# Laying out SBUF by hand in a two-layer streaming trunk, with every block chain of matmuls 256 columns wide

## The chip, the cores and the metric

The kernel runs on one core of a Trainium2 chip. The metric is the device time of one execution in microseconds. Of the kernel before there are three timed runs and one profiled execution.

## What is computed

The reference is a trunk of two layers over 512 tokens of width 1024, in float32. Layer A mixes tokens with a chunkwise mLSTM and a memory attention, layer B with a banded attention on a shared K/V projection and the memory attention. Each has a gated MLP with a depthwise convolution (inner width 2816) behind it.

```python
def conv_ffn(h, w_up, conv_w, conv_b, w_down):
    u, g = jnp.split(h @ w_up, 2, axis=-1)
    g = causal_dwconv(g, conv_w, conv_b)
    return (jax.nn.silu(g) * u) @ w_down

# layer A: x + [mlstm_chunkwise | memory_attention](rmsnorm(x) @ w_in) @ w_out
# layer B: x + [band_attention | memory_attention](rmsnorm(x) @ w_in) @ w_out, with one shared K/V projection
# each layer then: x + conv_ffn(rmsnorm(x)); after layer B a final rmsnorm
```

The change concerns the two MLPs most, since each has its matrix products done there in blocks of 256 tokens.

## The kernel before

**Number format.** Every matrix is split into a high part (a cast to fp32r on ScalarE, L130) and a low part (a subtraction on VectorE, L131). A product is three matmuls, high by high, high by low, low by high (`mm3`, L177, L178, L179). The weight, the stationary operand, is loaded into TensorE for every matmul; the activations move. In the profile's names `wh` and `wl` are the high and the low part of a weight, `u` is a tile of any split activation, query, block form or state, and `pmm`, `psc`, `ptr` are PSUM tiles.

**The channel mixer (the MLP).** It runs over 22 output tiles j of 128 features. Tiles 0 to 4 (`plain`) are 512 columns wide. Tiles 5 to 21 are written as `later()` and `step()`: a step computes the up and the gate product of one tile for both halves of the tokens with seven calls in place of eight, by sums and differences of weight quarters and of the token halves. The calls, in the order of the program, are a11, a12, s2, then one unit of down products, s1, s3, a second unit, a22, s4. A call has four k-tiles, each with three matmuls of 256 columns, so 12 matmuls. The stationary operands of a11 and a12 are the parts of the up weights (`split_up`), those of s1 and s3 the parts of sums (`split_sums`), all four in `wh` and `wl` tiles. Those of s2, a22 and s4 are "forms" (`form`), split into two tiles with the tag `u` each. A down unit has 12 matmuls of 512 columns into `ptr`. Steps 5 to 8 have one unit, 9 to 20 two, 21 none. There are 17 steps in each of the two layers, 34 in all.

**Wide steps.** In steps 9 to 20 (`WIDE`, 24 of the 34) the calls s2, s3 and a22 are done by `wide_products`: for each k one matmul of 256 columns with the low part (L792) and one of 512 columns with the high part (L793), whose moving operand is the high and the low half of the activation side by side. The half of the result that lies in columns 256 to 511 of the bank is added afterwards on VectorE (L829).

**Order.** In the block stages the order on PE, ACT and DVE is that in which `later` and `step` are written, pinned by a manual schedule. Elsewhere a scheduler orders instructions by priority, and tags with a number of buffers decide when a tile is free again: an allocation takes the next buffer of its tag in turn and waits until that buffer's last reader is done. The DMA loads are on SP's queue in program order.

**Places in SBUF.** The pool has a tag for each kind of tile: `wr` (raw weights, 3 of 4096 bytes a partition), `wh` and `wl` (3 each, D + 64 floats, that is 4352 bytes or 8.5 times 512), `u` (57 of 2048 bytes), `t`, `pt`, `s`, `rb`, `bias`. The up parts and the sums begin 16 floats (`SHIFT`, 64 bytes) into their tile. In the built program every moving operand of the block stages begins at the same place modulo 512 bytes. Counted from there, the stationary forms lie at 0, and the parts of up and sums at 64 or at 320: since a tile is 8.5 times 512 bytes long, neighbours of one tag differ by 256, and where `wh` lies at 64, its `wl` lies at 320, and the other way round. The down weights and the weights of the plain stage lie at 0 or 256.

The lines that the change and the prediction's steps touch: the pool's sizes (L82), `small` (L95), `weight_tiles` and `parts` (L150 to L161), `form`, `split_up` and `split_sums` (in `Forms`, L862 on), `sum_products` and `later` (L795 to L829), x's tiles (in `reload_x`, L423), and the queries of layer B.

## Time and profile before

| what | value |
|---|---|
| median of 3 runs (lowest to highest) | 1190.41 us (1190.38 to 1190.46) |
| the profiled execution's own time | 1191.35 us |
| its span (first to last instruction) | 1189.6 us |
| mean granted TensorE clock | 0.999 |
| block stage of layer A, first matmul to the end | 341.87 to 587.8 us |
| block stage of layer B | 900.6 to 1146.8 us |

The profile is of one execution, on its own clock from the first instruction of the span. A row of its groups has line, engine, operation, output <- inputs, shapes, how often it occurs, busy time in us, mean ns of one, and the time that the engine stood idle just before it, with what ended that. In a timeline row the first two numbers are start and duration in us. A matmul's duration holds its way through the array and overlaps the next one's, so what a matmul costs is the distance from its start to the next start.

### The profile page before, as it was taken

Reading aid. Unit: us, or ns where it says so; the run is one execution under the profiler, and the core shown is the slowest. Engines: PE = TensorE matmul, PEld = TensorE weight load, DVE = VectorE, ACT = ScalarE, POOL = GpSimd, SP = SyncE. Lnnn points to the kernel's source line nnn. Section 1 sums busy time; section 2 is a strip of 40 time slices with the busy share of each in tenths; the row PEclk is TensorE's granted clock in tenths of the full one; section 3 lists DMA queues with packets and bytes.
Section 4 is the critical chain, followed back from the end, with each engine's and each line's share of the span. In section 5 each row is a group of like instructions: output and inputs, shape, how many; then the busy total and the mean of one; then the engine's idle time right before and its main releaser. Section 6 shows DMA issues by size and latency. Waiting matters only on the chain.

```text
span 1189.6 us, 18184 instructions
## 1 busy us (share of the span) xinstructions
PE 1179.0 (99%) x6719; PEld 1032.1 (87%) x6719; DVE 961.9 (81%) x1760; ACT 723.6 (61%) x1294; POOL 130.0 (11%) x222
## 2 busy tenths in 40 slices
PE   9999999999999999999999999999999999999997
PEld 8988888888889988999888888888889988999986
DVE  6877688888978888888798888997896888888855
ACT  5648677655655555555576667776565655555545
POOL 1211201010021111111021000101001010111100
PEclk9999999999999999999999999999999999999999
DMA  8645313444266666666564313245326466665551
GB/s 283 212 114 133 93 55 80 146 142 135 87 160 159 158 162 158 154 145 132 145 197 131 89 53 102 70 131 184 117 89 152 107 141 142 142 141 137 123 159 71
DMA packets 200155, 158.61 MB, mean 133 GB/s; under 512 B 8344, under 2 KB 179838, under 8 KB 200066
## 3 DMA queue, kind: packets, MB, share of 16 engines
q1 hardware_dynamic: 183906, 119.74, 34.3%
q0 software_dynamic: 15584, 36.67, 15.3%
q8 instruction: 53, 0.87, 0.3%
q10 hardware_dynamic: 576, 1.05, 0.2%
q14 instruction: 36, 0.29, 0.1%
HBM read 128.89 MB, written 32.46 MB: 136 GB/s over the span
## 4 chain that ended last, share of the span: by engine, by line
PE 92%; ACT 3%; DVE 2%; DMA 2%; issue 0%; SPq 0%; POOL 0%; POOLq 0%; DVEq 0%; ACTq 0%
PE pmm L177 15%; PE pmm L178 15%; PE pmm L179 14%; PE ptr L178 6%; PE ptr L177 6%; PE ptr L179 6%; PE pmm L793 6%; PE psc L179 5%; PE psc L178 5%; PE psc L177 5%; PE pmm L792 3%; PE psc L527 2%; DMA wr<-in_mem_w_kv_dram 2%; PE ptr L1358 1%; PE ptr L1379 1%; PE ptr L1380 1%
## 5 line engine op out<-in xcount | busy, mean ns | idle before, releaser
L177 PE MATMUL pmm<-u,wh 128*128 128x512 f32 (+1 forms) x872 | 307.6, 353 | 0.3 <-ACT u L130 0.2
L179 PE MATMUL pmm<-u,wl 128*128 128x512 f32 (+1 forms) x872 | 304.7, 350 | 0.0
L178 PE MATMUL pmm<-u,wh 128*128 128x512 f32 (+1 forms) x872 | 304.6, 350 | 0.0
L131 DVE TENSOR_TENSOR wl<-wr,wh 128x1024 fp32r<-128x1024 f32 (+3 forms) x172 | 199.8, 1162 | 56.8 <-ACT wh L130 54.9
L130 ACT CAST wh<-wr 128x1024 fp32r<-128x1024 f32 (+3 forms) x172 | 171.8, 1001 | 98.4 <-PE pmm L178 44.3
L179 PEld LDWEIGHTS pmm<-u,wl 128*128 128x128 f32 x872 | 163.9, 188 | 21.0
L177 PEld LDWEIGHTS pmm<-u,wh 128*128 128x128 f32 x872 | 164.3, 189 | 18.5 <-ACT u L130 1.1
L178 PEld LDWEIGHTS pmm<-u,wh 128*128 128x128 f32 x872 | 164.2, 188 | 18.2 <-DVE u L131 0.5
L177 PE MATMUL ptr<-u,wh 128*128 128x512 f32 x272 | 106.7, 392 | 0.0
L178 PE MATMUL ptr<-u,wh 128*128 128x512 f32 x272 | 106.2, 390 | 0.0
L179 PE MATMUL ptr<-u,wl 128*128 128x512 f32 x272 | 106.0, 390 | 0.0
L761 POOL DMA_DIRECT2D xspill<-t x64 | 55.5, 867 | 454.2 <-ACT t L760 443.5
L130 ACT CAST u<-pt 128x512 fp32r<-128x512 f32 x102 | 62.7, 617 | 46.9 <-DVE pt L883 46.8
L131 DVE TENSOR_TENSOR u<-pt,u 128x512 fp32r<-128x512 f32 x102 | 69.9, 688 | 11.0 <-ACT u L130 8.3
L177 PE MATMUL psc<-u,wh 128*128 128x256 f32 (+1 forms) x232 | 75.9, 327 | 0.0
L179 PE MATMUL psc<-u,wl 128*128 128x256 f32 (+1 forms) x232 | 75.7, 326 | 0.0
L178 PE MATMUL psc<-u,wh 128*128 128x256 f32 (+1 forms) x232 | 75.6, 326 | 0.0
L793 PE MATMUL pmm<-u,u 128*128 128x512 f32 x192 | 69.9, 398 | 0.0
L945 ACT ACTIVATE t<-t 128x512 f32<-128x512 f32 x34 | 21.5, 633 | 79.4 <-DVE t L668 79.4
L829 DVE TENSOR_TENSOR t<-t,pmm 128x256 f32<-128x256 f32 x72 | 30.1, 419 | 41.8 <-ACT t L827 41.8
L760 ACT COPY t<-ptr 128x512 f32<-128x512 f32 x64 | 37.4, 585 | 42.9 <-PE ptr L179 42.8
L668 DVE SCALAR_TENSOR_TENSOR t<-t,cols,t 128x511 f32<-128x511 f32 x80 | 59.7, 746 | 3.7 <-ACT t L675 3.7
(300 smaller groups left out, 2670.6 us busy)
## 6 DMA issues: line engine op xcount, KB each, us to landing
wr<-in_ffn_w_up_dram SPq DMA_DIRECT2D x54, 512.0 KB, 4.2
wr<-in_ffn_w_down_dram SPq DMA_DIRECT2D x38, 512.0 KB, 4.1
pt<-in_ffn_w_up_dram SPq DMA_DIRECT2D x34, 512.0 KB, 6.4
xspill<-t POOLq DMA_DIRECT2D x64, 256.0 KB, 5.3
wr<-in_a_w_in_dram SPq DMA_DIRECT2D x20, 512.0 KB, 3.8
xspill<-u POOLq DMA_DIRECT2D x32, 256.0 KB, 2.7
u<-xspill SPq DMA_DIRECT2D x32, 256.0 KB, 4.8
wr<-in_w_kv_dram SPq DMA_DIRECT2D x12, 512.0 KB, 3.8
```

What stands on the lines that cost most here:

```text
L130: high = A.copy(hi, src) if on_act else V.tensor_copy(hi, src)
L131: low = V.tensor_tensor(out=lo, in0=src, in1=f(hi), op=ALU.subtract)
L177: nc.tensor.matmul(o, lh, rh, start=first, stop=False, skip_group_check=more)
L178: nc.tensor.matmul(o, lh, rl, start=False, stop=False, skip_group_check=more)
L179: nc.tensor.matmul(o, ll, rh, start=False, stop=last, skip_group_check=more)
L527: nc.tensor.matmul(o, a, b, start=first and i == 0, stop=i == 1)
L668: V.scalar_tensor_tensor(acc[:, n:], src[:, : S - n], self.fw[:, c * FT + j : c * FT + j + 1], acc[:, n:], op0=ALU.mult, op1=ALU.add,)
L760: A.copy(t, o)
L761: G.dma_start(xspill[j], t, accum_op=ALU.add)
L792: nc.tensor.matmul(r[:, :H], w[1][:, k], p[i - 1][:, :H], start=False, stop=False, skip_group_check=True)
L793: nc.tensor.matmul(r, w[0][:, k], p[i - 1], start=False, stop=k == n - 1, skip_group_check=True)
L829: V.tensor_tensor(out=o, in0=o, in1=r[:, H:], op=ALU.add)
```

## The change

Three things are changed together.

1. **Places.** The pool's tags are laid out in a fixed order (`sizes`, with one `first_` tile of each tag allocated ahead). `wh` and `wl` become six tags of one buffer each, `wh0` to `wh2` and `wl0` to `wl2`. Up parts always take block 0 and sums always block 1, both 16 floats in; all other weights take the next block in turn. The small vectors `s0` to `s3` lie between them and fill each block up to a multiple of 512 bytes. A new tag `f` of eight tiles takes the forms, the tiles of x (`xT`), the queries of layer B's first five head pairs and of one memory pair, which all had `u` tiles; `u` has 50 buffers instead of 57. In the built program the moving operands begin where they began modulo 512, and counted from there every stationary operand of the seven calls lies at 64, forms included, and those of the down and plain products at 0.
2. **Width.** `WIDE` and `wide_products` are gone: all seven calls of all 34 steps are 12 matmuls of 256 columns, with no addition on VectorE behind them. TensorE has 288 matmuls more (72 calls, 12 in place of 8), VectorE has 72 instructions fewer.
3. **Constants.** `ones` is the fp32r tile read as float32, and has no tile of its own.

```diff
@@ -44,7 +44,6 @@
 UNITS = {PLAIN - 1: (0, 1, 2, 3), 5: (None, 4), 6: (None, 5), 7: (None, 6), 8: (None, 7)}
 UNITS.update((j, (2 * j - 10, 2 * j - 9)) for j in range(9, 21))
 
-WIDE = range(9, 21)
 H = S // 2
 
 
@@ -79,7 +78,11 @@
     pool = ctx.enter_context(tc.tile_pool(name="pool", bufs=1))
     psum = ctx.enter_context(tc.tile_pool(name="psum", bufs=1, space=bass.MemoryType.PSUM))
 
-    bufs = {"wr": 3, "wh": 3, "wl": 3, "u": 57, "t": 8, "pt": 2, "s": 16, "rb": 3, "bias": 4}
+    HALF = 16
+    sizes = {"u": (50, S), "pt": (2, 5 * S), "wr": (3, D), "t": (8, S), "wh2": (1, D), "wl2": (1, D), "rb": (3, S)}
+    sizes.update({"bias": (4, S), "wh0": (1, D + HALF), "f": (8, S), "s0": (7, 16), "wh1": (1, D + HALF), "s1": (7, 16)})
+    sizes.update({"wl0": (1, D + HALF), "s2": (7, 16), "wl1": (1, D + HALF), "s3": (7, 16)})
+    bufs = {tag: n for tag, (n, _) in sizes.items()}
     pbufs = {"mm": 3, "sc": 3, "tr": 2}
     count = [0]
     dram = ctx.enter_context(tc.tile_pool(name="dram", bufs=1, space=bass.MemoryType.DRAM))
@@ -92,16 +95,23 @@
         count[0] += 1
         return psum.tile([P, S], F32, tag=tag, name=f"p{tag}{count[0]}", bufs=pbufs[tag])
 
-    def small(n=4):
-        return sb("s", [P, 32])[:, :n]
+    for tag, (n, size) in sizes.items():
+        pool.tile([P, size], F32, tag=tag, name=f"first_{tag}", bufs=n)
+
+    smalls = [0]
+
+    def small(n=4, dtype=F32):
+        smalls[0] += 1
+        return sb(f"s{smalls[0] % 4}", [P, 16], dtype)[:, :n]
 
 
     ident = cpool.tile([P, P], F32, name="ident")
     make_identity(nc, ident)
-    ones = cpool.tile([P, P], F32, name="ones")
-    V.memset(ones, 1.0)
     onesr = cpool.tile([P, P], F32R, name="onesr")
-    V.tensor_copy(onesr, ones)
+    once = sb("t", [P, P])
+    V.memset(once, 1.0)
+    V.tensor_copy(onesr, once)
+    ones = f(onesr)
     maskf = cpool.tile([P, P], F32, name="maskf")
     G.memset(maskf, 0.0)
 
@@ -145,18 +155,21 @@
             nc.sync.dma_start(raw[:, :, b:], extra)
         return raw
 
-    SHIFT = 16
-
-    def weight_tiles(a, b, at=0):
-        places = (at, at)
+    turn = [0]
+
+    def weight_tiles(a, b, block=None):
+
+
+        i, at = (turn[0] % 3, 0) if block is None else (block, HALF)
+        turn[0] = i + 1
         return [
-            sb(tag, [P, D + 64], F32R)[:, o : o + a * b].rearrange("p (a b) -> p a b", a=a)
-            for tag, o in zip(("wh", "wl"), places)
+            sb(f"{tag}{i}", [P, D + HALF * (i < 2)], F32R)[:, at : at + a * b].rearrange("p (a b) -> p a b", a=a)
+            for tag in ("wh", "wl")
         ]
 
-    def parts(raw, pinned=False, at=0):
+    def parts(raw, pinned=False, block=None):
         _, a, b = raw.shape
-        hi, lo = weight_tiles(a, b, at)
+        hi, lo = weight_tiles(a, b, block)
         split(hi, lo, raw, pinned=pinned)
         return hi, lo
 
@@ -231,7 +244,7 @@
 
     def diagonal(c):
 
-        cs = [sb("s", [P, 32], F32R)[:, :TT] for _ in range(2)]
+        cs = [small(TT, F32R) for _ in range(2)]
         split(*cs, c, on_act=False)
         dgs = []
         for c in cs:
@@ -398,7 +411,7 @@
         tp = ps(("sc", "tr")[j % 2])
         for T in range(TT):
             nc.tensor.transpose(tp[:, T * P : (T + 1) * P], xr[T][:, j * P : (j + 1) * P], ident)
-        xT.append(sb("u", [P, S]))
+        xT.append(sb("f", [P, S]))
         A.copy(xT[j], tp)
 
     acts, scaled_x = [], []
@@ -419,7 +432,7 @@
 
     def reload_x():
         for j in range(KT):
-            xT[j] = sb("u", [P, S])
+            xT[j] = sb("f", [P, S])
             tc.keep_in_program_order(nc.sync.dma_start(xT[j], xspill[j]))
 
     def value_weights(hf, u):
@@ -501,8 +514,8 @@
 
 
 
-    def head_queries(t, scale=1.0):
-        qs, ls = ([sb("u", [P, S], F32R) for _ in range(2)] for _ in range(2))
+    def head_queries(t, scale=1.0, tag="u"):
+        qs, ls = ([sb(tag, [P, S], F32R) for _ in range(2)] for _ in range(2))
         for h, r in enumerate(HEADS):
             G.memset(f(ls[h])[HEADS[1 - h], :], 0.0)
             A.activation(qs[h][r, :], t[r, :], AF.Copy, scale=scale)
@@ -549,13 +562,13 @@
         split(hi, lo, s)
         return hi, lo
 
-    def queries(o, row):
+    def queries(o, row, tag="u"):
 
         if row is None:
             return head_queries(o, HD**-0.5)
         q = sb("t", [P, S])
         V.scalar_tensor_tensor(q, o, HD**-0.5, row, op0=ALU.mult, op1=ALU.mult)
-        return head_queries(q)
+        return head_queries(q, tag=tag)
 
     def scores(outs, q, tsl, k, c):
 
@@ -785,13 +798,6 @@
 
             return [(p[i - 1][:, :H], p[i - 1][:, H:]) for p in self.sums]
 
-        def wide_products(self, r, w, i):
-
-            n = KT // 2
-            for k, p in enumerate(self.sums):
-                nc.tensor.matmul(r[:, :H], w[1][:, k], p[i - 1][:, :H], start=False, stop=False, skip_group_check=True)
-                nc.tensor.matmul(r, w[0][:, k], p[i - 1], start=False, stop=k == n - 1, skip_group_check=True)
-
         def later(self):
 
 
@@ -820,13 +826,8 @@
 
             def sum_products(o, r, w, i):
 
-                if j in WIDE:
-                    self.wide_products(r, w, i)
-                else:
-                    self.products(r, w, self.t(i))
+                self.products(r, w, self.t(i))
                 A.copy(o, r[:, :H])
-                if j in WIDE:
-                    V.tensor_tensor(out=o, in0=o, in1=r[:, H:], op=ALU.add)
 
             new = Tail(self, j)
             then(tail, "last_block", "first_tap")
@@ -875,7 +876,7 @@
             return t[:, :n], t[:, n:]
 
         def form(self, src):
-            hi, lo = (sb("u", [P, S], F32R).rearrange("p (a b) -> p a b", a=KT // 2) for _ in range(2))
+            hi, lo = (sb("f", [P, S], F32R).rearrange("p (a b) -> p a b", a=KT // 2) for _ in range(2))
             split(hi, lo, src)
             return hi, lo
 
@@ -895,10 +896,10 @@
             self.sub(self.halves(self.s13)[1], self.halves(self.up)[0], self.halves(self.gate)[0])
 
         def split_up(self):
-            self.a11, self.a12 = zip(*(self.halves(t) for t in parts(self.up, at=SHIFT)))
+            self.a11, self.a12 = zip(*(self.halves(t) for t in parts(self.up, block=0)))
 
         def split_sums(self):
-            self.s1, self.s3 = zip(*(self.halves(t) for t in parts(self.s13, at=SHIFT)))
+            self.s1, self.s3 = zip(*(self.halves(t) for t in parts(self.s13, block=1)))
 
         def sum_fourth(self):
             s2, s4 = self.halves(self.s24)
@@ -1320,7 +1321,7 @@
             w = sb("u", [P, S], F32R).rearrange("p (h c) -> p h c", h=4)
             split(w[:, :, :HD], w[:, :, HD:], tp[:, i * MEM : (i + 1) * MEM].rearrange("p (h c) -> p h c", h=4))
             v += [w[:, :2, :], w[:, 2:, :]]
-        q = queries((yield from project(b_w_in, j * P, act)), norm.row)
+        q = queries((yield from project(b_w_in, j * P, act)), norm.row, "f" if j < 5 else "u")
         qkv[j] = q, k, v
 
     def band_attention(j, q, k, v):
@@ -1382,7 +1383,7 @@
         mixes[j] = values(outs)
 
     def b_memory_queries(hp):
-        memq[hp] = queries((yield from project(b_w_in, AW + hp * P, act)), norm.row)
+        memq[hp] = queries((yield from project(b_w_in, AW + hp * P, act)), norm.row, "u" if hp else "f")
 
     qkv = {}
     outp = OutProjection(b_w_out, mixes, (0, 3, "mm"), (3, 5, "sc"))
```

On PE, call s3 of a wide step, the stationary in `wh` and `wl`, reads before:

```order
L792 MATMUL pmm_4172<-u_3264,wl_4104 128x256
L793 MATMUL pmm_4172<-u_3264,wh_4103 128x512
L792 MATMUL pmm_4172<-u_3318,wl_4104 128x256
L793 MATMUL pmm_4172<-u_3318,wh_4103 128x512
L792 MATMUL pmm_4172<-u_3376,wl_4104 128x256
L793 MATMUL pmm_4172<-u_3376,wh_4103 128x512
```

and the first half of the same call (k-tiles 0 and 1) reads now:

```order
L190 MATMUL pmm_4364<-u_3281,wh_4295 128x256
L191 MATMUL pmm_4364<-u_3281,wh_4295 128x256
L192 MATMUL pmm_4364<-u_3281,wl_4296 128x256
L190 MATMUL pmm_4364<-u_3335,wh_4295 128x256
L191 MATMUL pmm_4364<-u_3335,wh_4295 128x256
L192 MATMUL pmm_4364<-u_3335,wl_4296 128x256
```

Three matmuls of 256 columns stand where one of 256 and one of 512 stood; what precedes and follows the call is unchanged.

On ACT, at the entry of layer A's block stage, the casts of step 5's first operands stand like this before, with `wh698` the up weights, `wh700` the sums and `wh702` the down weights:

```order
L130 COPY wh698_3525<-wr694_3514 128x1024
L130 COPY u680_3437<-t669_3382 128x512
L760 COPY t685_3458<-ptr684_3445 128x512
L130 COPY u696_3520<-pt633_3220 128x512
L130 COPY u704_3538<-pt632_3219 128x512
L130 COPY u707_3550<-pt633_3220 128x512
L760 COPY t687_3474<-ptr686_3461 128x512
L130 COPY wh700_3529<-pt633_3220 128x1024
L760 COPY t691_3494<-ptr690_3481 128x512
L130 COPY wh702_3534<-wr695_3516 128x1024
L760 COPY t693_3510<-ptr692_3497 128x512
```

and like this now, with `wh1701` the sums, `wh2703` the down weights and `wh0699` the up weights:

```order
L140 COPY wh1701_3546<-pt634_3237 128x1024
L140 COPY f708_3567<-pt634_3237 128x512
L140 COPY wh2703_3551<-wr696_3533 128x1024
L773 COPY t688_3491<-ptr687_3478 128x512
L773 COPY t692_3511<-ptr691_3498 128x512
L140 COPY wh0699_3542<-wr695_3531 128x1024
L773 COPY t694_3527<-ptr693_3514 128x512
L838 COPY t713_3574<-pmm710_3571 128x256
```

The up weights' cast has moved behind the sums' and the down weights'; it is the last of the three now, and takes the block (`wh0`) whose buffer the down weights of the last plain tile had.

## The prediction, made before the result was known

> **What bounds the kernel now.** I read the busy times first, then the chain of work that ended last, both from the page.
>
> ```profile
> PE 1179.0 (99%) x6719; PEld 1032.1 (87%) x6719; DVE 961.9 (81%) x1760; ACT 723.6 (61%) x1294; POOL 130.0 (11%) x222
> PE 92%; ACT 3%; DVE 2%; DMA 2%; issue 0%; SPq 0%; POOL 0%; POOLq 0%; DVEq 0%; ACTq 0%
> ```
>
> TensorE is busy for 1179.0 of 1189.6 us and makes 92% of the chain. The windows view over the two block stages (first row layer A's, second layer B's) is sharper still:
>
> ```profile
> 341.87:587.80 245.93, 245.93 (x1627) 225.17 (x1626) 200.85 (x312) 141.10 (x243) 39.41 (x53) 1.00 0.63 147
> 900.60:1146.80 246.20, 246.20 (x1628) 225.36 (x1628) 201.64 (x312) 141.76 (x243) 24.70 (x29) 1.00 0.58 133
> ```
>
> PE is busy for all of the 245.93 and 246.20 us, at a granted clock of 1.00. So here time is the sum of the distances between matmuls, and only two things can change it: the pace of matmuls, or a new wait in front of one.
>
> **The paces of 256 columns.** The timeline of PE, in step 8 of layer A (a narrow step). The last call of the step ahead, s4 with stationary forms, begins with the first of these rows, a11 with the second, and s2 with the third:
>
> ```profile
> 378.57 0.28 PE L177 MATMUL psc<-u,u 128*128 128x256 f32 x1
> ...
> 380.01 0.28 PE L177 MATMUL pmm<-u,wh 128*128 128x256 f32 x1
> ...
> 382.84 0.28 PE L177 MATMUL pmm<-u,u 128*128 128x256 f32 x1
> ```
>
> The 12 matmuls of s4 take 1.44 us, 120 ns each. The 24 of a11 and a12 take 382.84 - 380.01 = 2.83 us, 117.9 each (with s2's entry left out 117.7, or 353 ns for a triple). The same two calls in step 20, behind a wide step (first a11's third k-tile, then the first row of s2):
>
> ```profile
> 561.81 0.28 PE L177 MATMUL pmm<-u,wh 128*128 128x256 f32 x1
> ...
> 563.85 0.28 PE L792 MATMUL pmm<-u,u 128*128 128x256 f32 x1
> ```
>
> 18 matmuls in 2.04 us are 113.3 each. One shape has three paces, then: 113.3, about 117.7 and 120. The groups of one window in the wide steps of layer A show the three as mean durations of 277, 281 and 284 ns, and so tell which call runs how (the first row is a11 and a12, the second s2 and a22, the third s4, the last s1):
>
> ```profile
> L177 PE MATMUL pmm<-u,wh 128*128 128x256 f32 x80 | 22.2, 277 | 0.0
> ...
> L792 PE MATMUL pmm<-u,u 128*128 128x256 f32 x73 | 20.5, 281 | 0.0
> ...
> L179 PE MATMUL psc<-u,u 128*128 128x256 f32 x40 | 11.3, 284 | 0.0
> ...
> L177 PE MATMUL psc<-u,wh 128*128 128x256 f32 x36 | 10.1, 281 | 0.0
> ```
>
> Forms (`u,u`, at distance 0 from the moving operand) run at 120. Parts in `wh` and `wl` (64 or 320 away) run at 117.7 in s1 of every step, whether `wh` lies at 64 and `wl` at 320 or the other way round. Only a11 and a12 behind a wide step, in the very places in which they lie in step 8, reach 113.3. **So distance 0 costs something, but distance 64 does not give the fast pace by itself**: the chain ahead decides it too, and behind a narrow s4, as all will be, the trace shows 117.7.
>
> A page of the Trainium skill speaks against a price of places at all. "SBUF — State Buffer", section "Who interferes with whom", gives TensorE one read port for the moving operand and an independent one for weight loads, and says that PE and ACT never wait on anyone. By that rule the three paces would have nothing to do with addresses; the trace's 120 beside 113.3 for one shape does not agree with an absence of interference, though it cannot tell places from a call's neighbours. What the rule would make of the sum is a rival below.
>
> **The change, term by term.** First the seven calls. A steady wide step and a narrow one, from a11's first row to the next step's:
>
> ```profile
> 561.12 0.28 PE L177 MATMUL pmm<-u,wh 128*128 128x256 f32 x1
> ...
> 576.41 0.28 PE L177 MATMUL pmm<-u,wh 128*128 128x256 f32 x1
> ```
>
> ```profile
> 392.72 0.28 PE L177 MATMUL pmm<-u,wh 128*128 128x256 f32 x1
> ```
>
> The wide step lasts 15.29 us; its first down unit goes from 565.26 to 568.00:
>
> ```profile
> 565.26 0.40 PE L177 MATMUL ptr<-u,wh 128*128 128x512 f32 x1
> ...
> 568.00 0.28 PE L177 MATMUL psc<-u,wh 128*128 128x256 f32 x1
> ```
>
> so two units take 5.48 and the calls 9.81. The narrow step (380.01 to 392.72) lasts 12.71, with one unit 9.97. After the change a step is 84 matmuls of 256 columns, and the pace is the whole question:
> - all at 117.7 ns: 9.89 us, +0.08 in 24 wide steps and -0.08 in 10 narrow ones (5 to 8 and 21 of each layer): 1.9 - 0.8 = **+1.1 us**
> - the 48 with `wh` and `wl` at 117.7, the 36 with forms still at 120: 9.97, so 24 x 0.16 = +3.8 us
> - all at 113.3: 9.52, so 24 x -0.29 + 10 x -0.45 = -11.5 us.
>
> I take the first. The forms move to the distance at which `wh` parts show 117.7; a11 and a12 lose the wide chain behind which they ran at 113.3, and the two nearly cancel. That every load of a chain now lies at 64, where one or two in three did before, should not matter, since both mixtures give the same 281. The first and the third bullet are also the ends of what a pure chain at 64, which this trace does not have, may do on the good side; the second is the end on the bad side.
>
> The VectorE additions that go (first row) took 72 x 419 ns:
>
> ```profile
> L829 DVE TENSOR_TENSOR t<-t,pmm 128x256 f32<-128x256 f32 x72 | 30.1, 419 | 41.8 <-ACT t L827 41.8
> ```
>
> They are worth nothing: PE has no idle time in these stages, and DVE is busy for 201 of 246 us. Without that cover each would be worth at most its 0.42 us.
>
> Second, a **new wait at layer A's entry**. Now up's parts must go to block 0, which the last plain tile's down weights hold. ACT's and DVE's casts and subtractions of weights, and PE, as they are before:
>
> ```profile
> 330.96 1.05 ACT L130 CAST wh<-wr 128x1024 fp32r<-128x1024 f32 x1 [0.19 <-PE psc L178]
> ...
> 341.85 1.05 ACT L130 CAST wh<-wr 128x1024 fp32r<-128x1024 f32 x1 [1.91 <-PE ptr L178]
> ```
>
> ```profile
> 342.93 1.23 DVE L131 TENSOR_TENSOR wl<-wr,wh 128x1024 fp32r<-128x1024 f32 x1 [3.48 <-ACT wh L130]
> ```
>
> ```profile
> 341.65 0.39 PE L179 MATMUL ptr<-u,wl 128*128 128x512 f32 x1
> 341.87 0.28 PE L177 MATMUL pmm<-u,wh 128*128 128x256 f32 x1
> 341.99 0.28 PE L178 MATMUL pmm<-u,wh 128*128 128x256 f32 x1
> 342.11 0.28 PE L179 MATMUL pmm<-u,wl 128*128 128x256 f32 x1
> ```
>
> Before, up is cast at 330.96, and it is the down weights, not needed for some 5 us, that wait until 341.85 for the last plain tile's down products. Now up waits there. Its high part is ready at 341.85 + 1.05 = 342.90, so a11 starts 1.03 us late; its low part at 342.93 + 1.23 = 344.16, and the third matmul, which needs it, started at 342.11: **+2.05 us** in all. Queued behind the waiting cast on ACT stand one copy of a down product and the copies of a11's result; nothing that PE needs sooner. In layer B the turn of the blocks is another: what held block 0 is read out some products before the entry, and I count 0. The ends are 0 (if the buffer is released one product earlier) and 2.3.
>
> Third, the rest: 50 `u` tiles instead of 57, x and queries in 8 `f` tiles, and loads of x further up on SP's queue. Where PE stands still before is short enough to list; the longest waits of the whole kernel, by the view of waits, are
>
> ```profile
> PE pmm L436 <- DVE mcf L117: 1.1, 1, 1.1
> PE ptr L400 <- ACT cols L328: 1.0, 1, 1.0
> ```
>
> The next is 0.3. So there is no existing stall that an earlier load could remove. What can come is a new one: the first queries of the mLSTM stage get their tiles later, when an x tile is released, layer B's queries from the third pair on reuse `f` tiles, and the scheduler shifts some rows there. ACT is busy for 61% and DVE for 81%, so most of it is covered; I put 0, with ends of -1 and +3 us. If the cover is gone, a late query holds up the scores behind it. At the ends of the layers the loads of x move behind two loads of weights; x was issued at 585.8, and its first reader stands at 594.56, so 5 us hide it:
>
> ```profile
> 585.81 3.81 SPq L423 DMA_DIRECT2D u<-xspill  x8
> ...
> 594.56 1.45 DVE L1281 TENSOR_TENSOR u<-u,pmm 128x512 f32<-128x512 f32 x2
> ```
>
> The sum: 1.1 + 2.05 + 0 = about +3.1 us. The profiled execution took 1191.35 us, 0.94 above the median of the runs; its span plus 1.75. From it I get 1194.5, and from the median 1190.41 + 3.1 = **1193.5 us**, which I give.
>
> **The rivals.**
>
> *A. The fast pace takes hold everywhere.* For: 113.3 is shown for these very places, it lasts through 18 matmuls and more once it is there, and the breaks that a 120 chain or a wide chain brings would be gone. Against: s1, entered from a down unit, is at 281 in all steps and never gets there, and all chains will be entered so. Price -11.5 + 2.05 = -9.5: 1180.9 us.
>
> *B. The fast pace takes hold in part*, as in a11 and a12 today (24 steps, 24 matmuls, 4.4 ns: 2.5 us kept): 3.1 - 2.5 = +0.6, or 1191.0; with a22 and s4, which share the chain, in 34 steps (34 x 24 x 4.4 ns = 3.6 us), and a11 and a12 in the 10 narrow ones (1.1 us), -4.1, some 1186.
>
> *C. Places do nothing*; each call keeps its pace by its kind (this is the rule cited above). Forms stay at 120, parts at 117.7, and the wide pairs, of which s3's and s2's four took about what 12 matmuls at 117.7 take, were the better trade: +3.8 + 2.05 = +5.9, so 1196.3 us. It is the nearer case once the forms run above 118.9, half way between 117.7 and 120.
>
> *D. The new tags run out.* A wait for an `f` or `u` tile on ACT in layer B or the mLSTM stage holds PE for some us on top of the forecast, 3 or more: 1197 to 1199.
>
> That the change doesn't do what it says is not one of them: in the order of the changed program all 34 steps have seven calls of 12 matmuls.
>
> **How the numbers follow.** The forecast has 0.42 (its own range 1191.5 to 1196), A 0.25, B 0.13, C 0.13, D 0.07. A measurement of this kernel can tell about 0.2%, 2.4 us: faster is below 1188.0, slower above 1192.8. Faster is A and half of B, 0.31; the same is the other half of B and the low part of the forecast's range (0.13), 0.2; slower is the rest, 0.49. The range goes from A with 1 us to spare to the low end of D: 1180 to 1197.
>
> **What would show it.** The groups of L190 to L192 of the changed kernel with 256 columns: means of 281 throughout confirm the forecast, 277 A, and 283 or 284 for `u,f` with 281 for `u,wh` C. A row of PE waits near 342 us, ended by ACT's cast of `wh0` and by DVE's `wl0`, of 1.0 and 1.1 us, confirms the entry. The forecast is wrong if chains at distance 64 alone hold the fast pace when entered from a down unit, which no row here can exclude.

## The result, and the profile after

The changed kernel takes 1195.95 us (median of 4 runs, 1195.0 to 1197.72), the kernel before 1190.39 us beside it: a ratio of 1.0049, with a 95% interval from 1.0032 to 1.0067. It is 5.6 us slower; the forecast was 3.1 us slower. Its profiled execution is the slowest of the four, with a span of 1196.0 us, 6.4 us above the one before.

The page's busy times and the shares of its chain say what they said before: TensorE is the bound.

```profile
PE 1182.7 (99%) x7007; PEld 1048.0 (88%) x7007; DVE 937.4 (78%) x1688; ACT 724.6 (61%) x1294; POOL 129.5 (11%) x222
PE 94%; DVE 3%; ACT 2%; issue 0%; DMA 0%; SPq 0%; POOL 0%; POOLq 0%; ACTq 0%; DVEq 0%
```

VectorE's busy time fell by 24.5 us (the 72 additions of 0.42 us, 30 us, and some work grown longer) and nothing came of it.

**The pace.** The groups of the seven calls in layer A's steps 12 to 20 (a11, a12 and s3 in the first row, then s2 and a22, s4, s1):

```profile
L190 PE MATMUL pmm<-u,wh 128*128 128x256 f32 x116 | 32.6, 281 | 0.0
...
L190 PE MATMUL pmm<-u,f 128*128 128x256 f32 x77 | 21.6, 281 | 0.0
...
L190 PE MATMUL psc<-u,f 128*128 128x256 f32 x40 | 11.2, 281 | 0.0
...
L190 PE MATMUL psc<-u,wh 128*128 128x256 f32 x36 | 10.1, 281 | 0.0
```

A mean duration of 281 ns is a distance of 117.7 ns from start to start. The forms came from 284 to 281, a11 and a12 went from 277 to 281: one pace in all seven calls, as forecast.

**The entry of layer A's block stage**, in PE's timeline. The first row is the last down product, the second waits for up's high part, the fourth for its low part:

```profile
341.23 0.39 PE L192 MATMUL ptr<-u,wl 128*128 128x512 f32 x1
342.52 0.39 PE L190 MATMUL pmm<-u,wh 128*128 128x256 f32 x1 [0.91 <-ACT wh L140]
342.74 0.28 PE L191 MATMUL pmm<-u,wh 128*128 128x256 f32 x1
343.78 0.58 PE L192 MATMUL pmm<-u,wl 128*128 128x256 f32 x1 [0.76 <-DVE wl L141]
344.16 0.42 PE L190 MATMUL pmm<-u,wh 128*128 128x256 f32 x1
...
347.15 0.31 PE L192 MATMUL pmm<-u,wl 128*128 128x256 f32 x1
347.30 0.28 PE L190 MATMUL pmm<-u,wh 128*128 128x256 f32 x1
```

Both waits are there, with the releasers and nearly the lengths of the forecast. But look at what follows: from 344.16 to 347.15 there are 14 matmuls 213 ns apart, before the distance falls to 118. The windows view over 341 to 348 us, in which the third number from the end is the granted clock, shows why:

```profile
341.00:348.00 7.00, 5.33 (x27) 4.71 (x26) 1.23 (x1) 1.90 (x3) 1.42 (x2) 0.76 1.04 225
```

The clock was 0.76 of full speed on the mean of these 7 us, where the same window before has 1.00: behind the second wait TensorE was granted half its clock for 3.4 us. No term of the prediction had that.

**Between the block stages.** The last matmul of layer A's stage and the first of layer B's stand in PE's timeline before at

```profile
587.52 0.28 PE L179 MATMUL psc<-u,u 128*128 128x256 f32 x1
...
900.64 0.28 PE L177 MATMUL pmm<-u,wh 128*128 128x256 f32 x1
```

and after at

```profile
591.52 0.28 PE L192 MATMUL psc<-u,f 128*128 128x256 f32 x1
...
906.35 0.28 PE L190 MATMUL pmm<-u,wh 128*128 128x256 f32 x1
```

That is 313.1 us before and 314.8 after, 1.7 us more for layer B's attention and what lies around it. These two landmarks and the last matmul ahead of the first stage cut every execution into parts (starts from PE's timeline; the run names are those of the next section):

| kernel | layer A's block stage with its entry | between | layer B's block stage |
|---|---|---|---|
| before | 245.87 | 313.13 | 245.84 |
| changed | 250.30 | 314.83 | 246.50 |
| entry_turn | 246.50 | 314.79 | 246.49 |
| after_wide | 248.30 | 314.83 | 246.33 |
| before_narrow | 247.79 | 313.03 | 247.76 |
| queries_in_u | 250.14 | 314.94 | 246.49 |
| scan_low | 251.07 | 315.08 | 247.33 |
| scan_high | 247.60 | 314.88 | 245.39 |
| split_places | 242.71 | 314.16 | 242.65 |
| high_low_apart | 241.13 | 314.27 | 241.10 |
| scan_fine | 248.31 | 315.05 | 248.30 |
| apart_u50 | 241.13 | 314.07 | 241.14 |
| apart_q2 | 241.17 | 314.11 | 241.15 |
| before_u53 | 247.03 | 314.47 | 246.98 |

From before to changed that is +4.4, +1.7 and +0.7; what lies ahead of the first stage is 0.4 us shorter, and the rest agrees within 0.1.

### The profile page after: what moved, and what is told of

Same layout as the page of the kernel before. It is cut to its first block, busy times and chain, and to the rows that moved or that the text cites. A ratio compares the mean times of both kernels' runs of the same rounds, so it can differ in the third digit from the quotient of the medians.

```text
span 1196.0 us, 18681 instructions
## 1 busy us (share of the span) xinstructions
PE 1182.7 (99%) x7007; PEld 1048.0 (88%) x7007; DVE 937.4 (78%) x1688; ACT 724.6 (61%) x1294; POOL 129.5 (11%) x222
## 4 chain that ended last, share of the span: by engine, by line
PE 94%; DVE 3%; ACT 2%; issue 0%; DMA 0%; SPq 0%; POOL 0%; POOLq 0%; ACTq 0%; DVEq 0%
PE pmm L190 18%; PE pmm L192 18%; PE pmm L191 18%; PE ptr L191 6%; PE ptr L190 6%; PE ptr L192 6%; PE psc L192 5%; PE psc L191 5%; PE psc L190 5%; PE psc L540 2%; PE ptr L1359 1%; PE ptr L609 1%; PE ptr L623 1%; PE ptr L1380 1%; PE ptr L1381 1%
## 5 line engine op out<-in xcount | busy, mean ns | idle before, releaser
L190 PE MATMUL pmm<-u,wh 128*128 128x512 f32 (+1 forms) x968 | 336.6, 348 | 1.2 <-ACT wh L140 0.9
L192 PE MATMUL pmm<-u,wl 128*128 128x512 f32 (+1 forms) x968 | 333.0, 344 | 0.8 <-DVE wl L141 0.8
L191 PE MATMUL pmm<-u,wh 128*128 128x512 f32 (+1 forms) x968 | 332.7, 344 | 0.0
L192 PEld LDWEIGHTS pmm<-u,wl 128*128 128x128 f32 x968 | 182.6, 189 | 22.3 <-DVE wl L141 1.0
L191 PEld LDWEIGHTS pmm<-u,wh 128*128 128x128 f32 x968 | 184.5, 191 | 18.3 <-DVE u L141 0.5
L190 PEld LDWEIGHTS pmm<-u,wh 128*128 128x128 f32 x968 | 182.6, 189 | 19.8 <-ACT wh L140 1.3
L141 DVE TENSOR_TENSOR f<-pt,f 128x512 fp32r<-128x512 f32 x102 | 70.1, 688 | 11.5 <-ACT f L140 8.9
L190 PE MATMUL pmm<-u,f 128*128 128x256 f32 x272 | 76.6, 282 | 0.0
L192 PE MATMUL pmm<-u,f 128*128 128x256 f32 x272 | 76.4, 281 | 0.0
L191 PE MATMUL pmm<-u,f 128*128 128x256 f32 x272 | 76.4, 281 | 0.0
L140 ACT CAST f<-pt 128x512 fp32r<-128x512 f32 x102 | 62.9, 617 | 13.6 <-DVE pt L884 13.3
L830 ACT COPY t<-pmm 128x256 f32<-128x256 f32 x102 | 37.3, 366 | 54.3 <-PE pmm L192 54.2
```

What stands on the lines that cost most here:

```text
L140: high = A.copy(hi, src) if on_act else V.tensor_copy(hi, src)
L141: low = V.tensor_tensor(out=lo, in0=src, in1=f(hi), op=ALU.subtract)
L190: nc.tensor.matmul(o, lh, rh, start=first, stop=False, skip_group_check=more)
L191: nc.tensor.matmul(o, lh, rl, start=False, stop=False, skip_group_check=more)
L192: nc.tensor.matmul(o, ll, rh, start=False, stop=last, skip_group_check=more)
L830: A.copy(o, r[:, :H])
```

## The experiments

Theory after the result: the pace went as forecast (+0.65 us a stage); the entry cost its stall of 2 us and about 1.7 us of slow clock behind it; layer B's attention lost 1.7 us to fewer or differently shared tiles. Rivals: the slow clock has nothing to do with the stall; the width, not the places, sets the pace; the tag of the queries, of x, or the number of `u` tiles delays layer B.

### The entry: entry_turn

```diff
-    turn = [0]
+    turn = [2]
```

Now block 0 holds weights that are read ahead of the last plain tile's down products, and its second down weights, which held block 0, lie in block 2.

> The changed kernel with one number altered: the blocks' turn starts at 2, so that the last plain tile's down weights lie in block 2 and block 0 is free when step 5's up weights are cast. Theory (the entry cost a stall of 1.7 us and then about 1.6 us at half the clock): TensorE goes from the last down product straight into a11, no matmul of 256 columns there takes over 125 ns, and the time falls by 3.0 to 3.6 us to about 1192.5. Rival (only the stall counts, the slow matmuls behind it would have come anyway): the time falls by 1.7 to 2.1 us to about 1194.

Measured: 1192.88 us (11 runs), ratio to before 1.0019, interval 1.001 to 1.0028, and 3.1 us less than the changed kernel. No wait is left at the entry, and the clock of the window is full:

```profile
341.00:348.00 7.00, 7.00 (x60) 6.91 (x60) 4.95 (x7) 3.56 (x8) 1.42 (x2) 1.00 1.06 235
```

By the table the entry cost 250.30 - 246.50 = 3.8 us in the profiled execution of the changed kernel. The stall took the clock with it: the theory held.

How much of it is the clock, two other runs tell that kept the stall. after_wide and scan_high (below) have the same two waits of 0.9 and 0.8 us, and their clock did not fall. With layer B's stage as the measure of a stage without an entry, the entry cost 248.30 - 246.33 = 2.0 us there and 2.2 in scan_high; in the changed kernel, queries_in_u and scan_low, all with a clock of 0.76, it cost 3.8, 3.65 and 3.7. So the stall is worth 2.0 to 2.2 us, as forecast, and the clock about 1.7 us more, in some executions and not in others.

Why only in some, the traces show. In all 14 of them the granted clock stays at full for a whole multiple of 3.413 us (99, 247, 248 or 343 to 348 times), so it can be taken to be set anew for each stretch of that length; where it fell behind the stall, it fell for one stretch. In the changed kernel both waits lie in one stretch (first row), in which TensorE was idle for 3.41 - 1.74 = 1.67 us, and the next stretch (second row) has a clock of 0.50:

```profile
340.38:343.79 3.41, 1.74 (x9) 1.00 (x7) 1.23 (x1) 1.53 (x2) 0.82 (x3) 1.00 1.01 232
343.79:347.20 3.41, 3.41 (x16) 3.41 (x17) 0.00 (x0) 0.37 (x1) 0.88 (x2) 0.50 1.00 167
```

queries_in_u and scan_low have the same, also with 1.67 us idle. In after_wide a boundary falls between the two waits, so that neither stretch has more than 0.91 us of idle time, and both, and the one behind them, have the full clock:

```profile
338.61:342.03 3.42, 2.51 (x12) 1.79 (x10) 0.30 (x1) 1.51 (x3) 0.85 (x1) 1.00 0.96 178
342.03:345.44 3.41, 2.65 (x23) 2.45 (x23) 0.92 (x1) 0.52 (x2) 1.42 (x2) 1.00 1.11 191
```

In scan_high the idle time is split 0.68 and 0.99. How much idle time it takes, the traces don't tell exactly: stretches with up to 1.31 us have no fall behind them, and neither has one with 1.71 us at the end of before_u53, with 15 matmuls in it where the three that were followed by a fall have 9 to 13. Half of 3.41 us is 1.7, which is what the fall cost. Where the boundaries lie changes from one execution to the next (the first change to the full clock comes 4.2 to 7.5 us into the span), so whether this stall pays for the clock is chance.

The Trainium skill, "TensorE: Matmul & The Clock Gate", section "What's actually happening", has the clock fall after an idle window of about 3.4 us, and says that the windows run free of the kernel. The free-running windows agree with these traces; that a window has to be idle as a whole does not, since 1.67 us in one was enough. The four timed runs of the changed kernel (1195.0, 1195.1, 1196.8, 1197.7) lie about as far apart as this, but of three of them there is no trace, so this is only likely.

### Width or place: after_wide and before_narrow

after_wide puts the wide steps back into the changed kernel, before_narrow takes them out of the kernel before:

```diff
+WIDE = range(9, 21)
...
+                if j in WIDE:
+                    self.wide_products(r, w, i)
+                else:
+                    self.products(r, w, self.t(i))
...
+                if j in WIDE:
+                    V.tensor_tensor(out=o, in0=o, in1=r[:, H:], op=ALU.add)
```

```diff
-WIDE = range(9, 21)
+WIDE = ()
```

> The changed kernel with the wide steps put back (L792, L793 and the VectorE additions), all places as changed. Theory (the pace is set by the chain ahead as well as by the place): a11 and a12 behind a wide step are at 113 to 115 ns again, the pairs of 256 and 512 columns at 353, s1 and s4 at 117.8: about 2 to 2.6 us faster than the changed kernel, about 1193.5. Rival (places alone set the pace): a11 and a12 stay at 117.8 and the time stays within 0.5 us of the changed kernel.

> The kernel before with the list of wide steps empty, all places as before. Theory: forms stay at 120 ns and parts of up and sums at 117.8, so 24 steps are 0.16 us longer each: 3.8 us above the kernel before, about 1194.2, with no wait at the entry. Rival (a chain that is narrow throughout settles at one pace whatever its places): forms at 117.8 too, and 1.0 us above the kernel before.

before_narrow: 1194.1 us (10 runs), 3.7 us above the kernel before by the medians (by the ratio, 1.0025 with 1.0016 to 1.0034, it is 3.0 us); +1.9 us in each stage and nothing elsewhere. Its groups in the same steps (a11, a12 and s3; s2 and a22; s4):

```profile
L177 PE MATMUL pmm<-u,wh 128*128 128x256 f32 x104 | 29.2, 281 | 0.0
...
L177 PE MATMUL pmm<-u,u 128*128 128x256 f32 x69 | 19.5, 283 | 0.0
...
L177 PE MATMUL psc<-u,u 128*128 128x256 f32 x32 | 9.1, 283 | 0.0
```

Forms at distance 0 stay at 283, 120 ns apart. With the changed places the same narrow chains run at 281. So the places gained what the second and the first bullet of the prediction differ by, and "places do nothing", rival C, is out, though its 1196.3 us is nearest to the time measured.

after_wide: 1196.15 us (4 runs), no different from the changed kernel's 1195.95. Here my theory fell: a11 and a12 stayed at 117.8 ns behind a wide step (in steps 9 to 20 each of the two calls takes 16.96 us a layer, 144 matmuls; at 113.3 it would be 16.3), and the rival's forecast came. But that places alone set the pace doesn't follow. The kernel before and before_narrow differ in width alone, and there a11 and a12 of steps 9 to 20 take 115.0 and 113.7 ns on the mean with the wide steps, 117.8 and 118.0 without. So on the old places the wide chain ahead is needed for the fast pace, and on the changed places it does not bring it. On the changed places width is worth next to nothing (246.33 and 246.50 us in layer B's stage), and the VectorE additions cost nothing.

### Which distance: scan_low, scan_high, scan_fine

In these only the offsets of the tiles are different (and `u` has 49 tiles, to pay for padding), for instance in scan_low:

```diff
-    HALF = 16
+    AT = {"wh0": 32, "wl0": 32, "wh1": 48, "wl1": 48, "wh2": 0, "wl2": 0}
+    FORM = 64
...
```

in floats of 4 bytes: 128 bytes for up, 192 for sums, 256 for forms. scan_fine has 8, 24 and 40, with x's tiles in `u`, and entry_turn's line.

> The changed kernel with other distances from the moving operand, counted in bytes modulo 512: parts of up (a11, a12) at 128, parts of sums (s1, s3) at 192, forms (s2, a22, s4) at 256; u has 49 tiles, since the padding takes the place of one. Theory (any distance but 0 gives the same mixture of collisions): all calls at 117.8 ns. Rival (distance matters by degrees): one of the three shows another pace, 113.3 at a distance at which a load never meets the moving reads, or up to 120.

> As the run with 128, 192 and 256, but parts of up at 320, parts of sums at 384, forms at 448. Theory: all calls at 117.8 ns. Rival: one of the three shows another pace, down to 113.3 or up to 120.

> The changed kernel with a free block 0 at the entry and finer distances: parts of up (a11, a12) at 32 bytes from the moving operand, sums (s1, s3) at 96, forms (s2, a22, s4) at 160; x's tiles are u tiles again, of which there are 49. Theory (the pace depends on the distance modulo 256, and 0 and 128 are the slow ends): 96 and 160 between 117.8 and 120 behind a down unit, none at 113.3 there. Rival (some distance between the multiples of 64 has no collision at all): one of them at 113.3 in s1 or a22. For layer B's attention: if x's tiles in f are what delays it by 1.6 us, it comes back to within 0.4 us of the kernel before; if it is the number of u tiles, it does not.

Times of one run each: 1198.5, 1193.2 and 1197.0 us. The distances from start to start, means of 12 matmuls over layer A's and B's steps 9 to 20, behind a down unit (d) or behind another call (c):

| distance in bytes | s1 or a22 (d) | calls behind another call (c) |
|---|---|---|
| 0 (before_narrow) | 119.4 | 119.7 to 120.0 |
| 32 | - | 118.5 to 118.8 |
| 64 (changed) | 117.8 | 117.8 |
| 96 | 117.4 | 117.5 |
| 128 | - | 118.2 to 118.5 |
| 160 | 120.0 | 119.2 to 119.5 |
| 192 | 117.8 | 117.6 |
| 256 | 119.4 | 120.0 |
| 320 | - | 114.8, then 113.3 |
| 384 | 120.6 | 120.2 |
| 448 | 117.8 | s4 117.5; s2 113.3 |

The paces behind a down unit run from 117.4 to 120.6, so "any distance but 0 gives 117.8" is out, and none of them is 113.3, so a distance that is free of any price is out too. Places matter by degrees: 0 and 256 are among the slowest, with 160 and 384, and 64, 96, 192 and 448 are the best. A pace that goes by the distance modulo 256, scan_fine's theory, does not hold either: 128 and 384 differ, 118.2 to 118.5 beside 120.2. Most distances were measured with one kind of weights only, 64 with all and 192 (below) with sums and forms. But scan_high has it: in a11 at 320 behind s4 at 448, in a12, and then in s2 at 448 again. Its groups (a11, a12 and s3 together; s2 and a22; s1; s4):

```profile
L195 PE MATMUL pmm<-u,wh 128*128 128x256 f32 x106 | 29.5, 278 | 0.0
L195 PE MATMUL pmm<-u,f 128*128 128x256 f32 x71 | 19.7, 277 | 0.0
...
L195 PE MATMUL psc<-u,wh 128*128 128x256 f32 x36 | 10.2, 283 | 0.0
...
L195 PE MATMUL psc<-u,f 128*128 128x256 f32 x32 | 8.9, 279 | 0.0
```

And scan_low has 113.3 in s1 at 192 of the steps that have no down unit ahead of it, where it follows s2 at 256, but 117.8 where it follows a down unit. The same distance, 192 or 448, holds either pace; **the pace of 113.3 can begin where the distance changes from one call to the next, and lasts up to the next down unit** (with one end seen before that: in scan_high's steps with one unit it ends at s1, where the distance goes from 448 to 384). That is the third theory, and it says what to build.

A change of the distance is not the only beginning. In the first step of after_wide, where everything lies at 64, the chain behind the two waits of the entry runs at 113.3 up to the down unit, and at 117.8 again behind it. Its s1 shows it, in a window over the rest of that step's calls:

```profile
L191 PE MATMUL psc<-u,wh 128*128 128x256 f32 x4 | 1.1, 276 | 0.0
```

queries_in_u has it in s1 and s3 of the same step; the changed kernel, with the same waits, runs these at 117.8. So place 64 does not hold a chain at 117.8: a down unit leaves it in that pace, and what stands at a stall can take it out as a change of distance can, but does not always.

### Changing the distance on purpose: split_places and high_low_apart

split_places has s1 and a22, the calls behind down units, at 192, and s4, a11, a12 and s2 at 64. s3, which was to lie at 64 too, lies at 320: by the edit the sums' second half begins 48 + 544 = 592 floats into its tile, 2368 bytes, which is 320 modulo 512. So s3 and s4 both follow a change, to two different distances. high_low_apart has every high part at 64 and every low part at 192. In both the forms use two tags of four tiles, `f` at 64 and `g` at 192, and entry_turn's line stays. high_low_apart's core:

```diff
+    UP, SUM, HALVES = (16, 48), (16, 48), (512, 512)
...
+    sizes.update({"bias": (4, S), "gap": (1, 16), "f": (4, S), "more": (1, 32), "g": (4, S), "fill": (1, 80)})
...
-            hi, lo = (sb("f", [P, S], F32R).rearrange("p (a b) -> p a b", a=KT // 2) for _ in range(2))
+            hi, lo = (sb(tag, [P, S], F32R).rearrange("p (a b) -> p a b", a=KT // 2) for tag in tags)
```

> The changed kernel with a free block 0 at the entry and two distances in each chain: s1 and a22, the calls behind a down unit, at 192 bytes from the moving operand, and s3, s4, a11, a12 and s2, the calls that follow them, at 64; u has 49 tiles. Theory (a chain that starts behind the down products settles at 117.8; when the distance then changes from 192 to 64, it falls into 113.3 within about three matmuls and stays there): s1 and a22 at 117.8, s3 and s4 at 114 to 115, a11, a12 and s2 at 113.3; 60 of 84 matmuls are 4.4 ns shorter in 34 steps, about 8.5 us less than the run with the block's turn altered: about 1184.5. Rival (the fast pace came from the particular distances 448 and 320 together): all calls at 117.8 and about 1193.

> The changed kernel with a free block 0 at the entry, every high part at 64 bytes from the moving operand and every low part at 192; u has 49 tiles. Theory (a change of distance lets a chain leave the slow state): every third load changes the distance, so all calls leave 117.8 soon after a down unit and run at 113.3, 84 matmuls 4.4 ns shorter in 34 steps: up to 12 us less than the run with the block's turn altered, about 1181. Rival (constant changes only make another mixture of collisions): 117 to 120 everywhere, 1192 to 1197.

split_places: 1185.7 us (4 runs), ratio to before 0.9956 (0.9939 to 0.9972). high_low_apart: 1182.02 us (4 runs), ratio 0.9924 (0.9909 to 0.9939), faster than both kernels. The groups of split_places show both paces side by side (a11, a12 and s3; s1; a22; s4; s2):

```profile
L206 PE MATMUL pmm<-u,wh 128*128 128x256 f32 x108 | 29.9, 277 | 0.0
...
L205 PE MATMUL psc<-u,wh 128*128 128x256 f32 x36 | 10.0, 279 | 0.0
...
L205 PE MATMUL pmm<-u,g 128*128 128x256 f32 x36 | 10.0, 279 | 0.0
...
L205 PE MATMUL psc<-u,f 128*128 128x256 f32 x36 | 10.0, 277 | 0.0
...
L205 PE MATMUL pmm<-u,f 128*128 128x256 f32 x33 | 9.1, 276 | 0.0
```

s1 and a22 are 117.5 ns from start to start, s3 and s4 114.8, a11, a12 and s2 113.3. In high_low_apart the timeline of one s1, from the last row of the down unit on, shows the chain going from 118 to 113 ns within itself:

```profile
562.05 0.39 PE L207 MATMUL ptr<-u,wl 128*128 128x512 f32 x1
562.27 0.28 PE L205 MATMUL psc<-u,wh 128*128 128x256 f32 x1
...
562.63 0.28 PE L205 MATMUL psc<-u,wh 128*128 128x256 f32 x1
...
562.98 0.28 PE L205 MATMUL psc<-u,wh 128*128 128x256 f32 x1
...
563.32 0.28 PE L205 MATMUL psc<-u,wh 128*128 128x256 f32 x1
...
563.65 0.28 PE L205 MATMUL pmm<-u,wh 128*128 128x256 f32 x1
```

The first triple takes 0.36 us, the next 0.35, then 0.34 and 0.33 (340 ns on the finer clock of the trace). A stage takes 241.1 us, 5.4 less than entry_turn's 246.5, twice.

### Layer B's attention: queries_in_u, apart_u50, apart_q2, before_u53

queries_in_u gives layer B's queries back to `u`; apart_u50 is high_low_apart with 50 tiles `u`; apart_q2 moves the queries of three pairs from `f` and `g` to `u` besides; before_u53 is the kernel before with one number altered:

```diff
-        q = queries((yield from project(b_w_in, j * P, act)), norm.row, "f" if j < 5 else "u")
+        q = queries((yield from project(b_w_in, j * P, act)), norm.row, "u")
...
```

```diff
-    bufs = {"wr": 3, "wh": 3, "wl": 3, "u": 57, "t": 8, "pt": 2, "s": 16, "rb": 3, "bias": 4}
+    bufs = {"wr": 3, "wh": 3, "wl": 3, "u": 53, "t": 8, "pt": 2, "s": 16, "rb": 3, "bias": 4}
```

> The changed kernel with layer B's queries back in u tiles (50 of them), so that only x and the forms use the tag f. Theory (layer B's attention loses 1.4 us because queries wait for f tiles): the waits of TensorE between 640 and 830 us return to those of the kernel before, and the time falls by 1.0 to 1.5 us to about 1194.7. Rival (the order there was shifted by the smaller number of u tiles, not by the queries' tag): no change, or slower, since u is now short by more.

> The run with high parts at 64 and low parts at 192, with 50 tiles u instead of 49 (three buffers of one small vector's tag instead of five). Theory (the number of u tiles is what delays layer B's attention): the attention takes 0.2 to 0.5 us less than with 49, total about 1181.7. Rival (it is the fixed sharing between u and the forms' tags): no change, 1182.0.

> As the run with 50 tiles u and high and low parts apart, but only the queries of layer B's first two pairs, not five, use the forms' tags; the rest use u. Theory (queries that wait for one of eight tiles delay the attention): 0.5 to 1 us less between 640 and 830 us, total about 1181. Rival (u is the scarcer tag): the attention loses a further 0.3 to 1 us, about 1182.5.

> The kernel before with 53 tiles u instead of 57, nothing else. Theory (fewer u tiles alone delay layer B's attention): 0.5 to 1.6 us more between 640 and 830 us than the kernel before, the block stages unchanged: about 1191 to 1192. Rival (four tiles fewer are covered): within 0.3 us there.

queries_in_u: 1196.36 us (4 runs) and 314.94 us between the stages, no better; scan_fine, with x in `u`, has 315.05, no better either. In both more tiles share `u`, so neither clears its tag by itself. before_narrow, with the old tiles and narrow chains, has 313.03, so the width is not it. before_u53 took 1194.3 us (one run); its landmarks

```profile
587.94 0.28 PE L179 MATMUL psc<-u,u 128*128 128x256 f32 x1
...
902.42 0.28 PE L177 MATMUL pmm<-u,wh 128*128 128x256 f32 x1
```

are 314.5 us apart, 1.3 more than before. **Fewer `u` tiles alone cost the kernel before most of what the changed kernel loses there (1.7 us).** They need not be all of it: split_places and high_low_apart, with 49 `u` tiles and the forms' tiles in two tags, have 314.16 and 314.27, some 0.6 us less than the changed kernel with its 50. apart_u50 (314.07; 1181.66 us, ratio 0.9928, 0.9916 to 0.994) has 0.2 us less than high_low_apart, no more than these parts differ among kernels that should be alike there, and the other sharing of the queries changes nothing (apart_q2, 314.11; 1181.57 us, ratio 0.9926, 0.9912 to 0.9939), against both of its expectations. Which tile is waited for between the stages was not found.

before_u53 also has 1.15 us more in each block stage, against its expectation, and there the trace shows the wait. In VectorE's waits in layer A's wide steps stands a row that the kernel before has not:

```profile
DVE u L131 <- PE ptr L178: 3.5, 3, 1.2
```

In steps 12, 16 and 20 of each layer the subtraction that writes a form's low part waits 1.2 us for a down product, which must be the last reader of the `u` buffer that it gets. VectorE is then late with the addition behind s3, a22 starts 0.2 us late and loses another 0.1 us in its first matmuls, and a11 and a12 of the next step run at 117.8 and 118.0 in place of 114.7 and 113.3, which is 0.1 us more: about 0.38 us three times a stage.

high_low_apart, apart_u50 and apart_q2 can't be told apart by their times; all are about 9 us faster than the kernel before and 14 us faster than the changed one.

## Why the prediction was right, and where it was not

- **The bound and the reading of paces** held: PE is the bound, time is the distance between matmuls, and 281 stands in every group.
- **The seven calls**: forecast +1.1 us by 117.7 ns everywhere, measured +0.63 and +0.65 in the two stages, 1.3 in sum (entry_turn against before). The argument that the loss of a11's and a12's fast pace would eat the gain of the forms was right in size and in sign. Its reason was half right: "the chain ahead decides it too" is shown by the scans, and before_narrow shows that on the old places the wide chain was needed; but it is not enough, since after_wide has the wide chain and not the pace.
- **The additions on VectorE**: worth nothing, as forecast.
- **The entry**: forecast +2.05 us by 1.03 and 1.1 us of waiting; the waits were 0.91 and 0.76 (the row's idle time leaves out the end of the matmul ahead), and the stall cost 2.0 to 2.2 us where the clock stayed up. The term was too small by what the stall does to the clock: about 1.7 us more in the profiled execution. The step that failed is the bound "2.3" of that term: it took for granted that matmuls behind a stall run at the pace of those before it.
- **The rest**, costed at 0 with ends of -1 and +3: +1.7 us in layer B's attention, inside the range, on its bad side. The step took from the busy shares of ACT (61%) and DVE (81%) that "most of it is covered". before_u53 shows that such shares tell nothing of cover: with four `u` tiles fewer VectorE waits 1.2 us at a time, and TensorE loses 1.3 us between the stages and 1.15 us in each.
- **The rivals**: A (all at 113.3) did not come, for the reason that the prediction gave against it: all chains are entered from a down unit, and at one distance nothing behind it starts the fast pace. Its price for the calls, -11.5 us, was nearly right: high_low_apart, with 113.3 in most calls and 115.1 in s1 and a22, has 9.5 us less in the two stages than the kernel before. C gave 1196.3, near the measured time, for a wrong reason: the forms did not stay at 120. The page that it rests on, the Trainium skill's "SBUF — State Buffer", section "Who interferes with whom", would have all distances alike; the scans' 117.4 to 120.6 ns by nothing but the place disagree with that.

So the 3.1 us were forecast out of two right terms. In the profiled execution, whose span grew by 6.4 us, the calls are 1.3, the stall 2.0 to 2.2, the clock behind it about 1.7, layer B's attention 1.7, and the part ahead of the first stage is 0.4 shorter. That the median of 1195.95 us lies within the forecast's own range, which ended at 1196, is luck: two of the four runs lie above it, the clock was not in the sum, and the tiles stood in it at 0.

## What to carry to other kernels

Where a matmul engine is the bound, read start-to-start distances by call, not busy shares: three paces of one shape were worth 11 us here (entry_turn against the alternating kernels), and a regular layout was not the fast one, an alternating one was. Give a stall in front of such an engine a price beyond its length, and look at the granted clock of the microseconds behind it. A pool from which a few buffers are taken for something else pays elsewhere, where nothing of the change is to be seen.

## What the runs showed of the hardware

- The pace of 256-column matmuls with a weight load each depends on where the weights lie relative to the moving operand: 117.4 to 120.6 ns for distances from 0 to 448 bytes behind a down unit. By the starts in the trace, a load begins 1 to 5 ns behind the matmul ahead in all chains, and its own matmul begins 110 ns later in chains at 113.3, 114 to 116 ns later at 117.8, and up to about 120 ns later in the slowest. Why it is later is not shown.
- The same distance holds two paces, 117.8 and 113.3. A change of the distance can start the pace of 113.3 (256 to 192, 448 to 320, 192 to 64, 192 to 320, or high and low parts 128 bytes apart), not every one does (256 to 128, and 0 to 64 behind a narrow chain, did not). Behind two waits of 0.91 and 0.76 us it began with everything at 64 in after_wide, and not in the changed kernel. A down unit of 512 columns ended it in every kernel; with high and low parts apart it was back within four triples.
- In these traces the granted clock stays at full for whole multiples of 3.413 us. A stretch of 3.41 us in which TensorE was idle for 1.67 us, with 9 to 13 matmuls in it, was followed by one at half the clock, in three executions of three. Where the same two waits fell into two stretches (0.91 and 0.76, or 0.68 and 0.99 us), the clock stayed at full, in two executions of two.
